# A hybrid SSD and attention layer: the scan's steps in three pieces, the norm per four chunks, GpSimd's products on VectorE and ScalarE

## The chip, the cores and the metric

The kernel runs on one core of a Trainium2 chip. The metric is the device time of one execution in microseconds (us). The engines are named as in the profile: PE is TensorE, DVE is VectorE, ACT is ScalarE, POOL is GpSimd, SP is SyncE, which issues most transfers. PE can run at two clocks, 1.2 and 2.4 GHz; the profile gives the granted clock as a share of the higher one.

## What is computed

One layer of a decoder for 512 tokens of width 1,024 in float32: a gated feed-forward, a mixer, a second gated feed-forward. The mixer projects the normed input once, onto the parts z, xBC and dt of a chunked state-space scan (SSD) and onto q, k and v of a differential attention; both results, side by side, go through an output projection. The change concerns the scan. It works on 4 chunks of 128 tokens, 2 groups of 8 heads of 64 columns:

```python
a_cs = jnp.cumsum(dt * a.reshape(g, hg), axis=2)
xdt = xs * dt[..., None]
seg = a_cs[:, :, :, None] - a_cs[:, :, None, :]
decay = jnp.where(causal, jnp.exp(jnp.where(causal, seg, 0.0)), 0.0)
cb = jnp.einsum("bcign,bcjgn->bcijg", cm, bm)
y_diag = jnp.einsum("bcijgh,bcjghp->bcighp", cb[..., None] * decay, xdt)
decay_states = jnp.exp(a_cs[:, :, -1:] - a_cs)
states = jnp.einsum("bclgn,bclgh,bclghp->bcghpn", bm, decay_states, xdt)
...
_, prev = lax.scan(step, h0, (jnp.moveaxis(states, 1, 0), jnp.moveaxis(chunk_decay, 1, 0)))
y_off = jnp.einsum("bclgn,bcghpn,bclgh->bclghp", cm, prev, jnp.exp(a_cs))
y = y_diag + y_off + xs * d_skip.astype(jnp.float32).reshape(g, hg)[:, :, None]
...
gated = (y_ssd * jax.nn.silu(z.astype(f32))).reshape(bsz, s, SSD_GROUPS, SSD_WIDTH // SSD_GROUPS)
y_ssd = rms_norm(gated, ssd_norm_w[l].reshape(SSD_GROUPS, -1)).reshape(bsz, s, SSD_WIDTH)
```

## The kernel before

Three stages follow each other: the first feed-forward, the mixer, and the second feed-forward. Every weight is split into a high and a low part when it is loaded: SP transfers a piece of 128x1024 (`raw`, three buffers), ACT rounds it to the high part (`whi`, L128), DVE subtracts to get the low part (`wlo`, L129), and a product takes three matmuls (high by high, high by low, low by high). `piece()` (L159) hands out the next piece and loads two ahead.

In the mixer, first the xBC columns are projected, convolved (DVE) and transposed (`conv_tr`). Then comes the stage that the change is about, from the first z matmul at 440 us to the first qk matmul at 581 us. In it PE works through eight projections of 256 columns (`tok_proj`, L590), four for z and four for v. Each has four units, one per block of 128 tokens, of 24 matmuls each, and yields after each unit. Two units share a PSUM bank (tag J, two banks); after the second, the callback empties the bank: for z ACT takes a tanh (L619) and a scaled copy (L620) per block and DVE a product (L621), for v ACT a scaled copy (L629) and DVE a subtraction (L630).

The scan has eight steps (chunk c, group g), the four chunks of group 0 first. They are laid between the units:

- `ssd_a` (L634): SP loads the cumulated decays of eight heads, spread over all partitions (`ab`, 128x8x128, three buffers, L639). PE makes C times B (L641), DVE masks it (`cbm`, L643). DVE subtracts and clamps the decay for each head (L645, eight instructions), ACT takes Exp of all of it (L647). POOL makes `xdt` (L650), the product of decay and `cbm` (L651), `xdd` (L655) and the skip product `y` (L657).
- `ssd_b` (L660): PE multiplies C with the running state (L666), DVE scales it (`yo`, L668), POOL adds it to `y` (L669). PE makes the chunk's state from `xdd` (L672), DVE updates the running state (L677, L678). PE makes the products within the chunk, eight heads (L680, into the other bank of the same tile `pd`), DVE adds `y` (L681) and multiplies with silu(z) (L683). Then comes the norm of this chunk: ACT squares and sums (L685), DVE takes the inverse root in a bit trick and three Newton rounds of three small instructions (`rsqrt`, L207, with L215 to L217) on one value per partition, and scales (L690).
- `ssd_c` (L693): PE transposes the step's result (`yt`, L697), ACT copies it (L698, one buffer), SP stores it in DRAM (`ysave`, L699). It is called one step after `ssd_b`; the last one after the first qk unit (`last_ssd`).

The list `plan` (L702) says within which projection a step stands; `ssd_a` of a step stands just ahead of `ssd_b` of the step before. The order of instructions on each engine is not simply that of the text: the kernel is built with `schedule_with_timeline_sim=True`, and a planner takes what is next in the text and, where its own estimate of times says that this isn't ready yet, something later that is. Each engine then works in that fixed order. After the stage the pools of the scan are closed, and the attention's tiles take their place in SBUF; the first is the square of the qk projection (L749).

## Time and profile before

| | us |
|---|---|
| median of 3 runs | 1207.35 |
| lowest, highest run | 1206.51, 1207.97 |
| span of the profiled execution, first to last instruction | 1203.1 |
| PE busy | 1163.4 |
| DVE busy | 926.0 |
| ACT busy | 533.8 |
| POOL busy | 210.6 |
| transferred | 119.56 MB, 99 GB/s on average |

The profile is of one execution; its own time on the device is not given apart from its span, and the runs are 3.4 to 4.9 us longer than the span. The page lists busy times over the whole span. PE is at 97% of it, but its records are modelled and overlap, so a full PE is not PE at its peak. The sections on stages are read from windows of the trace, in us from the start of the span. An idle time of an engine is put down to the instruction whose end released it.

### The profile page before, as it was taken

The numbers are of one execution on the slowest core, as the hardware profiler recorded it, in microseconds if no ns is written. First come the engines' busy times: TensorE is split into PE (matmuls) and PEld (weight loads), VectorE is DVE, ScalarE is ACT, GpSimd is POOL, SyncE is SP. The second block draws the span as 40 slices with busy tenths as digits, with TensorE's granted clock in tenths as the row PEclk, the third lists the DMA queues.
The fourth block names the chain that finished last, engine by engine and source line by source line (L and its number), as shares of the span: only waits on it lengthen the run. The fifth ranks groups of instructions, "written<-read, shape, count | busy, mean of one in ns | idle before, by whom it ended". The sixth has DMA issues, their size and how long they took to land.

```text
span 1203.1 us, 19035 instructions
## 1 busy us (share of the span) xinstructions
PE 1163.4 (97%) x7483; PEld 1036.3 (86%) x7483; DVE 926.0 (77%) x1593; ACT 533.8 (44%) x863; POOL 210.6 (18%) x214
## 2 busy tenths in 40 slices
PE   8999999999989999798999998899999999999998
PEld 6889999999967788797998886688789999999997
DVE  6988787787585867989588989636499988787862
ACT  5534343433352355343366675735244443434331
POOL 1000000000031004443255756315100000000000
PEclk9999999999998999899999999999999999999999
DMA  7223333333353224242321102216312333333332
GB/s 231 86 75 97 110 110 97 99 107 88 97 193 114 77 82 140 81 131 73 105 71 36 58 32 76 75 44 209 98 62 89 109 121 100 101 107 102 96 114 83
DMA packets 42393, 119.56 MB, mean 99 GB/s; under 512 B 4608, under 2 KB 9920, under 8 KB 42304
## 3 DMA queue, kind: packets, MB, share of 16 engines
q1 hardware_dynamic: 41024, 114.15, 30.3%
q0 software_dynamic: 1280, 4.20, 1.0%
q8 instruction: 59, 0.97, 0.3%
q14 instruction: 30, 0.25, 0.1%
HBM read 112.00 MB, written 6.32 MB: 98 GB/s over the span
## 4 chain that ended last, share of the span: by engine, by line
PE 40%; DVE 10%; issue 2%; ACT 2%; POOL 1%; DMA 0%; DVEq 0%; ACTq 0%; POOLq 0%
PE s L327 5%; PE s L326 5%; PE s L328 5%; PE dn L170 3%; PE dn L172 3%; PE dn L171 3%; PE wo L170 2%; PE wo L171 2%; PE wo L172 2%; DVE nmx L813 2%; DVE pe L823 1%; PE gu L170 1%; PE gu L172 1%; PE gu L171 1%; DVE wlo L129 1%
## 5 line engine op out<-in xcount | busy, mean ns | idle before, releaser
L129 DVE TENSOR_TENSOR wlo<-raw,whi 128x1024 fp32r<-128x1024 f32 (+3 forms) x225 | 225.9, 1007 | 120.0 <-ACT whi L128 104.4
L128 ACT CAST whi<-raw 128x1024 fp32r<-128x1024 f32 (+2 forms) x204 | 175.7, 865 | 310.2 <-PE s L327 121.7
L327 PE MATMUL s<-al,whi 128*128 128x256 f32 x952 | 265.2, 280 | 0.0
L326 PE MATMUL s<-ah,whi 128*128 128x256 f32 x952 | 263.6, 279 | 0.0
L328 PE MATMUL s<-ah,wlo 128*128 128x256 f32 x952 | 262.6, 279 | 0.0
L327 PEld LDWEIGHTS s<-al,whi 128*128 128x128 f32 x952 | 178.7, 188 | 2.1
L326 PEld LDWEIGHTS s<-ah,whi 128*128 128x128 f32 x952 | 178.5, 188 | 2.0
L328 PEld LDWEIGHTS s<-ah,wlo 128*128 128x128 f32 x952 | 177.2, 187 | 0.1
L170 PE MATMUL dn<-h,whi 128*128 128x512 f32 x352 | 137.6, 394 | 0.0
L172 PE MATMUL dn<-h,wlo 128*128 128x512 f32 x352 | 137.5, 392 | 0.0
L171 PE MATMUL dn<-h,whi 128*128 128x512 f32 x352 | 136.9, 389 | 0.0
L128 ACT CAST whi<-tw 128x1024 fp32r<-128x1024 f32 x68 | 70.3, 1049 | 141.2 <-PE s L327 65.7
L129 DVE TENSOR_TENSOR wlo<-tw,whi 128x1024 fp32r<-128x1024 f32 x68 | 82.1, 1220 | 2.8 <-ACT whi L128 2.5
L172 PEld LDWEIGHTS dn<-h,wlo 128*128 128x128 f32 x352 | 66.1, 188 | 14.6
L171 PEld LDWEIGHTS dn<-h,whi 128*128 128x128 f32 x352 | 66.1, 188 | 12.7
L170 PEld LDWEIGHTS dn<-h,whi 128*128 128x128 f32 x352 | 66.1, 188 | 12.2
L603 PE MATMUL qk<-whi,xhm 128*128 128x256 f32 x256 | 73.3, 287 | 1.1 <-DVE l L820 1.1
L605 PE MATMUL qk<-whi,xlm 128*128 128x256 f32 x256 | 72.8, 285 | 0.0
L604 PE MATMUL qk<-wlo,xhm 128*128 128x256 f32 x256 | 72.7, 284 | 0.0
L362 DVE SCALAR_TENSOR_TENSOR x<-dn,x 128x512 f32<-128x512 f32 x64 | 44.0, 688 | 35.4 <-PE dn L172 34.9
L170 PE MATMUL gu<-xh,whi 128*128 128x512 f32 x160 | 64.9, 406 | 2.7 <-POOL whi L126 1.7
L419 POOL DMA_DIRECT2D xsave<-x x8 | 4.6, 578 | 337.3 <-DVE x L362 337.3
(293 smaller groups left out, 2650.8 us busy)
## 6 DMA issues: line engine op xcount, KB each, us to landing
raw<-in_gu SPq DMA_DIRECT2D x86, 512.0 KB, 3.6
raw<-in_dn SPq DMA_DIRECT2D x48, 384.0 KB, 3.2
raw<-in_wqk SPq DMA_DIRECT2D x16, 512.0 KB, 3.6
raw<-in_wxbc SPq DMA_DIRECT2D x12, 512.0 KB, 3.5
raw<-in_wo SPq DMA_DIRECT2D x10, 512.0 KB, 4.1
raw<-in_dn SPq DMA_DIRECT2D x16, 256.0 KB, 2.7
raw<-in_wz SPq DMA_DIRECT2D x8, 512.0 KB, 3.5
ab<-acs_d SPq DMA_DIRECT2D x8, 512.0 KB, 4.1
```

Of the source, the lines that this page charges most:

```text
L128: S.copy(hi[:, a:b], raw[:, a:b])
L129: V.tensor_sub(lo[:, a:b], raw[:, a:b], hi[:, a:b].bitcast(F32))
L170: PE.matmul(ps, lhsT=hi, rhs=xh, start=start, stop=False)
L171: PE.matmul(ps, lhsT=hi, rhs=xl, start=False, stop=False)
L172: PE.matmul(ps, lhsT=lo, rhs=xh, start=False, stop=stop)
L326: PE.matmul(ps, lhsT=hi, rhs=ah[:, i, a], start=i == 0, stop=False)
L327: PE.matmul(ps, lhsT=hi, rhs=al[:, i, a], start=False, stop=False)
L328: PE.matmul(ps, lhsT=lo, rhs=ah[:, i, a], start=False, stop=i == 3)
L362: V.scalar_tensor_tensor(x[d], ps, 0.5, x[d], op0=ALU.mult, op1=ALU.add)
L603: PE.matmul(o, lhsT=xh, rhs=hi, start=k == 0, stop=False)
L604: PE.matmul(o, lhsT=xh, rhs=lo, start=False, stop=False)
L605: PE.matmul(o, lhsT=xl, rhs=hi, start=False, stop=k == KD - 1)
```

## The change

It leaves the mathematics as it is and touches the stage in four ways.

1. `ssd_b` becomes `ssd_o` (product with the state, state update), `ssd_d` (products within the chunk, product with silu(z), sum of squares) and `ssd_n` (norm). A loop over the eight steps runs `ssd_o`, one unit, `ssd_a` of the next step, one unit, `ssd_d`, one unit. Ahead of it stand four units, behind it the remaining four.
2. The norm is taken once per group, after its fourth chunk: one inverse root of four values per partition, and four scalings. The transposes of group 0 come in rounds 5 and 6 of the loop, counted from 0, two chunks in each, those of group 1 in `last_ssd`. `yt` has two buffers.
3. POOL has no work in the stage any more: `xdt`, the decay product, `xdd` and the sum of `y` and `yo` go to DVE. The skip product goes to ACT as eight scaled copies of 128x64. The subtraction and clamp of the decay go from DVE to ACT as eight Relus of the negated difference, and Exp takes the negative of that.
4. The projections are taken in the order z0, z1, v0, z2, z3, v1, v2, v3, and their weights are loaded in that order.

Lines of the text (comments and docstrings) that are removed elsewhere stand for nothing in the program and are left out here.

```diff
@@ -103,8 +103,8 @@
     mixp = [(wxbc[t], 1024) for t in (8, 9, 10, 11)]
     mixp += [(wdt, 128)]
     mixp += [(wxbc[t], 1024) for t in range(8)]
-    mixp += [(wz[g, i], 1024) for g in range(4) for i in range(2)]
-    mixp += [(wv[g, i], 1024) for g in range(4) for i in range(2)]
+    for w, g in ((wz, 0), (wz, 1), (wv, 0), (wz, 2), (wz, 3), (wv, 1), (wv, 2), (wv, 3)):
+        mixp += [(w[g, i], 1024) for i in range(2)]
     mixp += [(wqk[h, i], 1024) for h in range(8) for i in range(2)]
     for ds in ((0, 1), (2, 3), (4, 5)):
         mixp += [(wo[d, 0], 1024) for d in ds] + [(wo[d, 1, :, 0:512], 512) for d in ds]
...
@@ -631,7 +631,10 @@
                                        h.bitcast(F32), op0=ALU.mult, op1=ALU.subtract)
         return tok_proj(f"v{g}", cb)
 
+    ssq = [ssd.tile([P, NB], F32, name=f"ssq{g}") for g in range(2)]
+
     def ssd_a(c, g):
+
         hs = slice(g * 8, g * 8 + 8)
         sh = [P, 8, 64]
         cs = slice(c * P, (c + 1) * P)
...
@@ -642,31 +645,34 @@
         cbm = sb.tile([P, P], F32, tag="cbm", name="cbm")
         V.tensor_mul(cbm, pcb[:, :P], triu)
         for h in range(8):
-            V.tensor_scalar(ab[:, h, :], ab[:, h, :], acs[:, c, g * 8 + h:g * 8 + h + 1], 0.0,
-                            op0=ALU.subtract, op1=ALU.min)
-        S.activation(ab, ab, AF.Exp)
+            S.activation(ab[:, h, :], ab[:, h, :], AF.Relu, bias=acs[:, c, g * 8 + h:g * 8 + h + 1], scale=-1.0)
+        S.activation(ab, ab, AF.Exp, scale=-1.0)
         xg = sview(xs[:, c, g * 512:(g + 1) * 512])
         xdt = sb.tile(sh, F32, tag="xdt", name="xdt")
-        G.tensor_tensor(xdt, xg, dts[:, c, hs].unsqueeze(2).to_broadcast(sh), op=ALU.mult)
-        G.tensor_tensor(ab, ab, cbm.unsqueeze(1).to_broadcast([P, 8, P]), op=ALU.mult)
+        V.tensor_tensor(xdt, xg, dts[:, c, hs].unsqueeze(2).to_broadcast(sh), op=ALU.mult)
+        V.tensor_tensor(ab, ab, cbm.unsqueeze(1).to_broadcast([P, 8, P]), op=ALU.mult)
         xdd = None
         if c < NB - 1:
             xdd = sb.tile(sh, F32, tag="xdd", name="xdd", bufs=1)
-            G.tensor_tensor(xdd, xdt, dsd[:, c, hs].unsqueeze(2).to_broadcast(sh), op=ALU.mult)
+            V.tensor_tensor(xdd, xdt, dsd[:, c, hs].unsqueeze(2).to_broadcast(sh), op=ALU.mult)
         y = sb.tile(sh, F32, tag="y", name="y")
-        G.tensor_tensor(y, xg, row[:, R_DS + g * 8:R_DS + g * 8 + 8].unsqueeze(2).to_broadcast(sh), op=ALU.mult)
+        for h in range(8):
+            S.activation(y[:, h, :], xg[:, h, :], AF.Copy, scale=row[:, R_DS + g * 8 + h:R_DS + g * 8 + h + 1])
         return ab, xdt, xdd, y
 
-    def ssd_b(c, g, m, xdt, xdd, y):
+    pds = {}
+
+    def ssd_o(c, g, m, xdt, xdd, y):
+
         hs = slice(g * 8, g * 8 + 8)
         sh = [P, 8, 64]
         cs = slice(c * P, (c + 1) * P)
-        pd = pA(f"pd{c}{g}")
+        pd = pds[c, g] = pA(f"pd{c}{g}")
         if c > 0:
             PE.matmul(pd[:, 1, :], lhsT=cT[:, g, cs], rhs=state[:, g, :], start=True, stop=True)
             yo = sb.tile(sh, F32, tag="yo", name="yo", bufs=1)
             V.tensor_tensor(yo, sview(pd[:, 1, :]), ea[:, c, hs].unsqueeze(2).to_broadcast(sh), op=ALU.mult)
-            G.tensor_add(y, y, yo)
+            V.tensor_add(y, y, yo)
         if c < NB - 1:
             pst = pM(f"st{c}{g}")
             PE.matmul(pst, lhsT=btok[:, c, g, :], rhs=xdd.rearrange("p a b -> p (a b)"), start=True, stop=True)
...
@@ -676,22 +682,30 @@
             else:
                 V.tensor_tensor(st, st, cdec[:, c, hs].unsqueeze(2).to_broadcast(sh), op=ALU.mult)
                 V.tensor_add(st, sview(pst), st)
+
+    def ssd_d(c, g, m, xdt, xdd, y):
+
+        pd = pds.pop((c, g))
         for h in range(8):
             PE.matmul(pd[:, 0, h * 64:(h + 1) * 64], lhsT=m[:, h, :], rhs=xdt[:, h, :], start=True, stop=True)
         V.tensor_tensor(y, sview(pd[:, 0, :]), y, op=ALU.add)
         zt = sview(sz[:, c, g * 512:(g + 1) * 512])
         V.tensor_mul(zt, zt, y)
-        ss = tiny.tile([P, 1], F32, tag="ss", name=f"ss{c}")
-        S.activation(y, zt, AF.Square, accum_out=ss)
-        V.tensor_scalar(ss, ss, 1.0 / 512, EPS, op0=ALU.mult, op1=ALU.add)
-        rr = tiny.tile([P, 1], F32, tag="ssr", name="ssr")
-        rsqrt(rr, ss, [P, 1], "s")
+        S.activation(y, zt, AF.Square, accum_out=ssq[g][:, c:c + 1])
+
+    def ssd_n(g):
+
+        ss = tiny.tile([P, NB], F32, tag="ss", name=f"ss{g}")
+        V.tensor_scalar(ss, ssq[g], 1.0 / 512, EPS, op0=ALU.mult, op1=ALU.add)
+        rr = tiny.tile([P, NB], F32, tag="ssr", name="ssr")
+        rsqrt(rr, ss, [P, NB], "s")
         sl = slice(g * 512, (g + 1) * 512)
-        V.scalar_tensor_tensor(sz[:, c, sl], sz[:, c, sl], rr, row[:, R_SN + g * 512:R_SN + (g + 1) * 512],
-                               op0=ALU.mult, op1=ALU.mult)
+        for c in range(NB):
+            V.scalar_tensor_tensor(sz[:, c, sl], sz[:, c, sl], rr[:, c:c + 1], row[:, R_SN + g * 512:R_SN + (g + 1) * 512],
+                                   op0=ALU.mult, op1=ALU.mult)
 
     def ssd_c(c, g):
-        yt = sb.tile([P, 4, P], F32, tag="yt", name="yt", bufs=1)
+        yt = sb.tile([P, 4, P], F32, tag="yt", name="yt")
         pt = pM(f"yt{c}{g}")
         for i in range(4):
             PE.transpose(blk(pt, i), sz[:, c, g * 512 + i * P:g * 512 + (i + 1) * P], ident)
...
@@ -699,40 +713,48 @@
         nc.sync.dma_start(ysave[:, g * 4:g * 4 + 4, c, :], yt)
 
     steps = [(c, g) for g in range(2) for c in range(NB)]
-    plan = [[], [], [0, 1], [2], [3], [4, 5], [6], [7]]
-    fills = [z_group(g) for g in range(4)] + [v_group(g) for g in range(4)]
-    st_a = {}
-    done_c = [0]
-
-    def drain_c(upto):
-        while done_c[0] < upto:
-            ssd_c(*steps[done_c[0]])
-            done_c[0] += 1
-
-    for n, fill in enumerate(fills):
-        next(fill)
-        if n == 0:
-            for t, dst in last_conv:
-                conv_tr(t, dst)
-            cv_cm.__exit__(None, None, None)
-            sb_cm = tc.tile_pool(name="ssdb", bufs=2)
-            sb = sb_cm.__enter__()
-            next(fill)
-            st_a[0] = ssd_a(*steps[0])
-            st_a[1] = None
-        for s in plan[n]:
-            next(fill, None)
-            if st_a.get(s + 1) is None and s + 1 < 8:
-                st_a[s + 1] = ssd_a(*steps[s + 1])
-            ssd_b(*steps[s], *st_a[s])
-            drain_c(s)
-        for _ in fill:
-            pass
-    last_ssd = lambda: drain_c(8)
-
-    # ---------------- attention ----------------
+    units = [z_group(0), z_group(1), v_group(0), z_group(2), z_group(3), v_group(1), v_group(2), v_group(3)]
+
+    def unit(n=1):
+
+        while n and units:
+            try:
+                next(units[0])
+                n -= 1
+            except StopIteration:
+                units.pop(0)
+
+    unit()
+    for t, dst in last_conv:
+        conv_tr(t, dst)
+    cv_cm.__exit__(None, None, None)
+    sb_cm = tc.tile_pool(name="ssdb", bufs=2)
+    sb = sb_cm.__enter__()
+    unit()
+    ops = ssd_a(*steps[0])
+    unit(2)
+    for n, s in enumerate(steps):
+        ssd_o(*s, *ops)
+        unit()
+        nxt = ssd_a(*steps[n + 1]) if n < 7 else None
+        unit()
+        ssd_d(*s, *ops)
+        ops = nxt
+        if s[0] == NB - 1:
+            ssd_n(s[1])
+        if n in (5, 6):
+            for c in (0, 1) if n == 5 else (2, 3):
+                ssd_c(c, 0)
+        unit()
+    unit(32)
+
+    def last_ssd():
+        for c in range(NB):
+            ssd_c(c, 1)
+
+
     def rsqrt_act(dst, v, shape):
-        """dst = v ** -0.5: exp(-ln(v) / 2) and a Newton step."""
+
         y = tiny.tile(shape, F32, tag="ra_y", name="ra_y")
         t = tiny.tile(shape, F32, tag="ra_t", name="ra_t")
         S.activation(y, v, AF.Ln)
```

## Rows read from the trace of the kernel before

**Rows 1.** Page, part 1: busy us, share of the span and instructions by engine.
```profile
PE 1163.4 (97%) x7483; PEld 1036.3 (86%) x7483; DVE 926.0 (77%) x1593; ACT 533.8 (44%) x863; POOL 210.6 (18%) x214
```

**Rows 2.** Windows of the SSD stage: length, busy us by engine, granted clock, DMA.
```profile
440.00:581.00 141.00, 126.55 (x988) 119.32 (x987) 115.89 (x250) 57.37 (x103) 53.79 (x37) 0.96 0.31 100
...
440.00:475.00 35.00, 33.59 (x287) 32.53 (x285) 27.39 (x50) 20.11 (x35) 12.37 (x10) 1.00 0.29 96
...
510.00:545.00 35.00, 33.96 (x275) 31.85 (x274) 29.45 (x77) 17.10 (x30) 15.83 (x11) 1.00 0.37 114
```

**Rows 3.** Waits of PE, 440 to 581: us in total, times, longest.
```profile
PE yt L697 <- DVE sz L690: 8.1, 4, 4.1
PE pd L680 <- DVE yo L668: 4.9, 1, 4.9
PE z L603 <- ACT sz L620: 1.3, 1, 1.3
```

**Rows 4.** Windows of one wait and the stretch behind it (columns as in rows 2).
```profile
482.75:487.65 4.90, 0.01 (x2) 0.01 (x1) 4.90 (x10) 0.49 (x1) 3.34 (x2) 0.99 0.00 0
487.65:492.00 4.35, 4.35 (x20) 4.35 (x21) 4.28 (x8) 3.90 (x7) 2.24 (x2) 0.50 0.02 4
```

**Rows 5.** Timeline, 542 to 556: start, us, instruction, [idle before <-releaser].
```profile
542.08 0.68 DVE L668 TENSOR_TENSOR yo<-pd,ea 128x512 f32<-128x512 f32 x1
542.17 2.38 POOL L651 TENSOR_TENSOR ab<-ab,cbm 128x1024 f32<-128x1024 f32 x1 [1.86 <-DVE rs_t L215]
542.68 2.42 DVE L677 TENSOR_TENSOR state<-state,cdec 128x512 f32<-128x512 f32 x1
543.03 1.89 PE L680 MATMUL pd<-xdt,ab 128*128 128x64 f32 x16
...
556.09 0.38 PE L641 MATMUL cb<-cT,bT 128*128 128x128 f32 x2
```

**Rows 6.** Groups by line on DVE, 440 to 581: count | busy us, mean ns | idle before.
```profile
L645 DVE TENSOR_SCALAR ab<-ab,acs 128x128 f32<-128x128 f32 x64 | 26.1, 469 | 3.0 <-DMA ab<-acs_d 3.0
L129 DVE TENSOR_TENSOR wlo<-raw,whi 128x1024 fp32r<-128x1024 f32 x16 | 19.4, 1220 | 3.5 <-ACT whi L128 3.5
L215 DVE TENSOR_TENSOR rs_t<-rs_y 128x1 f32<-128x1 f32 x21 | 10.2, 485 | 0.5
...
L216 DVE SCALAR_TENSOR_TENSOR rs_t<-rs_t,ss 128x1 f32<-128x1 f32 x21 | 7.1, 337 | 0.4
L217 DVE SCALAR_TENSOR_TENSOR rs_y<-rs_t,rs_y 128x1 f32<-128x1 f32 x14 | 7.1, 504 | 0.2
...
L683 DVE TENSOR_TENSOR sz<-sz,y 128x512 f32<-128x512 f32 x8 | 5.7, 710 | 0.2
```

**Rows 7.** One line on DVE: count, shortest/median/longest ns, first and last start.
```profile
L215 DVE TENSOR_TENSOR rs_t<-rs_y x33: 145/160/2092, 29.0 to 863.9; 128x1 f32<-128x1 f32 x24, 128x4 f32<-128x4 f32 x9
```

**Rows 8.** Groups by line on POOL, 440 to 581 (columns as in rows 6).
```profile
L651 POOL TENSOR_TENSOR ab<-ab,cbm 128x1024 f32<-128x1024 f32 x8 | 20.5, 2569 | 22.1 <-DVE cbm L643 9.0 <-DVE rs_t L216 5.1 <-ACT ab L647 5.1
```

**Rows 9.** Groups by line on ACT, 440 to 600 (columns as in rows 6).
```profile
L128 ACT CAST whi<-raw 128x1024 fp32r<-128x1024 f32 x17 | 17.7, 1047 | 8.1 <-PE v L605 6.2 <-PE xbc L171 1.9
...
L629 ACT ACTIVATE vh<-v,rm 128x256 fp32r<-128x256 f32 x16 | 7.5, 471 | 16.8 <-DVE vl L630 12.2 <-PE v L605 4.6
```

**Rows 10.** Timeline of ACT, two instructions in a row (columns as in rows 5).
```profile
452.44 0.48 ACT L619 ACTIVATE th<-z,hr 128x256 f32<-128x256 f32 x1
452.81 0.48 ACT L620 ACTIVATE sz<-z,hr 128x256 f32<-128x256 f32 x1
```

**Rows 11.** Window of four z units without a wait (columns as in rows 2).
```profile
454.06:465.05 10.99, 10.99 (x96) 10.99 (x97) 10.99 (x23) 5.85 (x9) 6.87 (x5) 1.00 0.62 207
```

**Rows 12.** Timeline of SP's queue: the last issue for the scan.
```profile
533.58 0.33 SPq L639 DMA_DIRECT2D ab<-acs_d  x1
```

**Rows 13.** Page, part 6: DMA issues, KB each, median us to landing.
```profile
ab<-acs_d SPq DMA_DIRECT2D x8, 512.0 KB, 4.1
```

**Rows 14.** Timeline of ACT after the stage (columns as in rows 5).
```profile
593.38 0.60 ACT L749 ACTIVATE sqk<-qk 128x512 f32<-128x512 f32 x1 [1.14 <-DMA ysave<-yt]
```

## The prediction

> **What bounds the kernel now.** I read the page first: TensorE is busy 97% of the span [rows 1], so a change pays only where PE waits or runs slowly. All that is changed lies between the first z projection (440 us) and the first qk projection (581 us), so the second view is the window of those 141 us [rows 2]: PE is busy 126.55 us of it, idle 14.45, and its granted clock is 0.96 on average. The third view says what ended the idle time [rows 3]. 8.1 us of PE's waits are transposes of the normed scan output (yt, L697) that wait for the norm's last product on DVE (L690); 4.9 us are the intra-chunk products (pd, L680), put down to DVE's read of the inter-chunk product (yo, L668); 1.3 us are z matmuls that wait for ACT to empty their bank. A wait costs twice: in the 4.9 us of that pd wait PE does nothing while DVE works throughout, and in the 4.35 us behind it the granted clock is 0.50, the 1.2 GHz level, until it is back at 2.4 [rows 4].
>
> Why DVE is late shows in the timeline [rows 5]. While GpSimd multiplies the decay matrix (L651, 2.38 us from 542.17), DVE's L668, which reads PSUM, takes its 0.68 us, but L677, the same size with both inputs in SBUF, takes 2.42 and ends with GpSimd's instruction. The groups say the same of the sums [rows 6, 7]: L215, two SBUF inputs of one element per partition, has a median of 160 ns and a mean of 485; L645's mean is 469 ns for 128 elements, when a product of 512 (L683) takes 710. So the scan's steps hang on a busy DVE that GpSimd holds up, and PE waits at the end of that chain.
>
> **The change, part by part.** The matmuls and transposes are the same in number and shape, so PE's own work stays. What can be won is the idle time and the slow clock: 14.45 us, and 141 x 0.04 = 5.6 us of clock, together **20.1 us**.
>
> GpSimd's five products of a step leave it. DVE takes xdt (8), xdd (6) and y+yo (6), 20 products of 128x512 at L683's 0.71 us = 14.2 us, and the decay product, 8 at 1.22 us (L129, the same size, both inputs in SBUF) = 9.8 us [rows 6]; on GpSimd the latter took 2.57 [rows 8]. Together +24.0 us on DVE.
>
> The subtract-and-clamp of the decay (L645, 64 pieces, 26.1 us) leaves DVE; ACT does it as 64 Relus, and takes the skip product y as 64 copies of 128x64 with a scale. No row shows ACT at these sizes with a per-partition operand from SBUF alone. From L629 (256 elements, 471 ns) and L128 (1,024 elements, 1,047 ns) an element costs 0.75 ns [rows 9], so the far end is 375 ns for 128 and 327 ns for 64. The near end: of two instructions in a row the second starts 0.37 us after the first, which lasts 0.48 [rows 10], so 0.11 us less, 265 and 217 ns. ACT gains 64 x 0.48 = 31 us at the near end, 64 x 0.70 = 45 at the far end; I take the near one, since the eight stand in a row. ACT's 57.4 us become 88 (102 at the worst) [rows 2]; in some 125 us that is 71 to 82%.
>
> By the rows the Relu is no longer on ACT than its predecessor on DVE, 265 to 375 ns against L645's mean of 469 [rows 6], and it lands on the engine with room. A rule of the Trainium skill speaks against the move: "ScalarE: Activation LUTs", section Rules for kernel authors, wants relu on VectorE, up to about three times as fast per element in bf16. The trace doesn't agree in f32; by that factor the sum would be a slowdown (last rival).
>
> The norm is taken per four chunks: seven of the eight Newton chains lie in the stage, 10.2 + 7.1 + 7.1 us in the three groups of [rows 6]. Two chains stay, nine instructions each at the median 160 ns [rows 7], 2.9 us: -21.5 us. The four scalings with L690 stay. DVE's sum: 115.9 - 26.1 - 21.5 + 24.0 = 92 us, 74% of 125 where it was 82%, and nothing locks it out any more, since GpSimd has no work left in the stage.
>
> Now the waits. The transposes of the first group move two steps behind their norm, those of the second behind all of v3; the 8.1 us go. pd comes two projection units behind yo; four units last 10.99 us without a wait, so one lasts 2.75 [rows 11], and 5.5 us cover yo's 0.68 [rows 5]: the 4.9 us go. What is late next is ACT: its z and v banks (the 1.3 us) and the decay chain. What stays of idle time I take from the two quarters of the stage that have no long wait: 1.41 and 1.04 us in 35 [rows 2], 1.23 on average, so 4.4 us in 125. Both ends: nothing stays, or the rivals below.
>
> New waits and what is queued behind them. On SP the four transfers of ysave for the second group come together behind v3's weights. The copies have two buffers where they had one, so the third copy waits on ACT for the first transfer, and ACT's first qk squares stand behind it; they wait for the last transfer already now, and start at 593.38 [rows 14], 12.4 us after the stage. After the change: a qk unit 2.75, then twice a copy (0.6) and a transfer (at most the 4.1 of a larger one [rows 13]), 12.2 us. No change, and PE has four qk units (11 us) and two more under it; if that cover fails, the loss is the difference, under 1 us. The transfer of the decay rows (ab) is issued as soon as one of three buffers is free: the last at 533.58 [rows 12], 22.5 us ahead of its step's first product at 556.09 [rows 5]; I cost it at nothing. The regrouped weight order moves no transfer by more than some units; nothing.
>
> The sum: -14.45 - 5.6 + 4.4 = **-15.7 us**. The profiled execution has a span of 1203.1 us; the median of the runs is 1207.35, 4.25 above, for what lies around it. 1207.35 - 15.7 = 1191.7.
>
> **The rivals.**
> ACT late with the banks (1200 us). In a step ACT has, in one block, 8 Relus, Exp (1.05, as L128's size) and 8 copies, 4.9 to 6.7 us, and at a group's start two weight casts, 2.1: 7.0 to 8.8 us in which no bank is emptied. PE covers two units, 5.5, and the scan's own products, 1.9 (pd) to 2.3: 7.4 to 7.8. So 0 to 1.4 us a step, up to 11 in eight steps, with slow clock behind some: 1187.3 + 11 + 2 = 1200. For it: the 1.3 us of today. Against: the planner puts ready work between. Chance 0.14.
>
> The split does not take effect (1199 us). The order on each engine is the planner's, not the text's; it may bring pd next to yo again. Then only the norm's waits go, and 4.9 us with 2.2 of slow clock [rows 4] stay: 1191.7 + 7.1. Against: DVE is lighter. Chance 0.07.
>
> Slower (1222 us): the state update waits for xdd. In the text DVE's order is xdt, decay product, xdd, and the decay product waits for Exp and that for eight Relus; the state matmul of the step needs xdd. Now GpSimd has that order in its own queue, and none of PE's waits is for it [rows 3]. From Relu to xdd: 2.1 to 3.0 + 1.05 + 1.22 + 0.71 = 5.1 to 6.0 us; behind four bank reads (1.5) and two casts (2.1) 8.7 to 9.6. The cover to the state matmul is unit, pd, unit: 2.75 + 1.89 + 2.75 = 7.4. So 1.3 to 2.2 us a step, in six steps; if the ab transfer is late as well, its 4.1 come on top, 5.4 to 6.3, some 35 us: 1207.35 - 20.1 + 35 = 1222. It decides from 20.1 / 6 = 3.35 us a step on. Against: the transfer's lead of 22.5 us, and that Relus can start as soon as it has landed. Chance 0.10.
>
> ACT as the bound (1234 us). If a Relu took three times L645's 0.469 us, 1.41, the 64 would need 90 us and ACT 57.4 + 90 + 21 (copies at the far end) = 168 us, 27 more than the stage has now: 1207.35 + 27. It decides from 0.8 us a Relu on, where ACT passes the stage's 125 us. Against: both ends for a Relu, 0.265 and 0.375. Chance 0.01. That is what the rule on relu in "ScalarE: Activation LUTs" would come to.
>
> **How the numbers follow.** Forecast 0.66, ACT late 0.14, split undone 0.07, slower 0.11 (0.10 and 0.01), about as before 0.02. The likeliest gives 1191.7. The low end is the whole 20.1 us, 1187; the high end takes in the second and third case, 1202. Beyond it lie the slower cases and the worst of ACT. A measurement here can tell 0.2% (2.4 us) from no change: faster 0.84, same 0.05, slower 0.11.
>
> **What would show it.** Right: the stage from the first z to the first qk matmul is 124 to 127 us long, PE's idle time in it under 6 us, its granted clock 0.99 or 1.00; no wait of the yt transposes for the norm; GpSimd empty; DVE's Newton steps at about 0.16 us on average; ACT between 85 and 102 us. Wrong: PE waits for z or v banks that ACT empties, for xdd or the decay product, with clock at 0.50 behind; or Relus over 0.4 us a piece; or qk products that wait for ysave's transfers.

## The result and the profile after

| | before | after |
|---|---|---|
| median of 4 runs, us | 1206.93 | 1195.41 |
| lowest, highest run | 1206.06, 1207.97 | 1191.88, 1196.45 |
| profiled execution: span (time) | 1203.1 | 1192.3 (1194.4) |
| first z to first qk matmul ("scan") | 140.21 | 121.31 |
| first qk to first matmul of the second feed-forward ("attention") | 273.58 | 281.01 |

The ratio of the runs is 0.9899, with a 95% interval of 0.9882 to 0.9917: faster by 1.0%, inside the range, 3.7 us above the forecast of 1191.7. The two lower lines tell more than the sum: the scan got 18.9 us shorter, and the attention, whose text the change doesn't touch, got 7.4 us longer.

The page after, part 1, answers to [rows 1]: DVE and POOL lost 31 and 55 us of work, ACT gained 36.

```profile
PE 1160.0 (97%) x7483; PEld 1033.1 (87%) x7483; DVE 895.1 (75%) x1485; ACT 569.6 (48%) x991; POOL 155.2 (13%) x178
```

The windows of the two stretches; first the attention before, then both after (columns as in [rows 2]):

```profile
580.84:854.42 273.58, 260.62 (x1735) 226.62 (x1733) 201.51 (x401) 159.00 (x375) 133.60 (x129) 0.99 0.26 81
```

```profile
441.33:562.64 121.31, 119.40 (x977) 112.95 (x976) 87.30 (x154) 89.61 (x231) 0.00 (x0) 1.00 0.34 109
562.64:843.65 281.01, 263.53 (x1739) 229.23 (x1738) 199.22 (x388) 161.32 (x375) 132.59 (x129) 0.99 0.25 81
```

In the scan PE's idle time fell from 14.45 to 1.91 us, its clock is 1.00 throughout, and POOL has nothing to do, against 53.8 us in [rows 2]. In the attention PE's idle time rose from 12.96 (273.58 - 260.62) to 17.48 us, and its busy time from 260.6 to 263.5, though of matmuls only four more transposes of the scan's result lie in it (eight instead of four).

PE's waits in the scan after (us in total, times, longest), against [rows 3]:

```profile
PE pd L690 <- DVE ab L653: 0.8, 1, 0.8
PE z L603 <- ACT sz L620: 0.7, 1, 0.7
PE st L678 <- ACT sz L620: 0.4, 1, 0.4
```

The transposes' 8.1 us and the 4.9 us of pd behind yo are gone; what is left are three short waits. The groups on DVE and on ACT in the same stretch (columns as in [rows 6]):

```profile
L653 DVE TENSOR_TENSOR ab<-ab,cbm 128x1024 f32<-128x1024 f32 x8 | 9.8, 1222 | 5.1 <-ACT ab L649 5.0
...
L215 DVE TENSOR_TENSOR rs_t<-rs_y 128x4 f32<-128x4 f32 x6 | 1.0, 161 | 0.2
```

```profile
L648 ACT ACTIVATE ab<-ab,acs 128x128 f32<-128x128 f32 x64 | 20.4, 416 | 0.3 <-DMA ab<-acs_d 0.3
...
L660 ACT ACTIVATE y<-xs,row 128x64 f32<-128x64 f32 x64 | 16.7, 355 | 0.1
```

L215 has a mean of 161 ns where [rows 6] had 485 (there on one value per partition, which takes 156 ns in move_only below). An instruction of DVE that lasts longer while POOL works is called held from here on. The decay product takes 1.22 us where GpSimd took 2.57 [rows 8]. The Relus last 416 ns each but 20.4 us together, so they start 0.32 us apart on average; the scaled copies 355 ns and 0.26.

### The profile page after: what moved, and what is told of

It reads as the page before. It is cut to its first block, busy times and chain, and to the rows that moved or that the text cites. A ratio compares the mean times of both kernels' runs of the same rounds, so it can differ in the third digit from the quotient of the medians.

```text
span 1192.3 us, 18991 instructions
## 1 busy us (share of the span) xinstructions
PE 1160.0 (97%) x7483; PEld 1033.1 (87%) x7483; DVE 895.1 (75%) x1485; ACT 569.6 (48%) x991; POOL 155.2 (13%) x178
## 4 chain that ended last, share of the span: by engine, by line
PE 83%; DVE 8%; ACT 4%; issue 2%; POOL 1%; DMA 1%; SPq 0%; ACTq 0%; POOLq 0%; DVEq 0%
PE s L327 9%; PE s L326 9%; PE s L328 9%; PE dn L170 6%; PE dn L172 6%; PE dn L171 6%; PE gu L170 3%; PE gu L172 3%; PE gu L171 3%; PE wo L172 2%; PE wo L170 2%; PE wo L171 2%; PE xbc L170 2%; PE xbc L171 2%; PE xbc L172 2%
## 5 line engine op out<-in xcount | busy, mean ns | idle before, releaser
L128 ACT CAST whi<-raw 128x1024 fp32r<-128x1024 f32 (+2 forms) x204 | 176.6, 868 | 309.5 <-PE s L327 121.7
L171 PEld LDWEIGHTS dn<-h,whi 128*128 128x128 f32 x352 | 66.1, 188 | 12.7
L170 PEld LDWEIGHTS dn<-h,whi 128*128 128x128 f32 x352 | 66.1, 188 | 12.2
L172 PE MATMUL gu<-xh,wlo 128*128 128x512 f32 x160 | 63.7, 398 | 0.0
```

Of the source, the lines that this page charges most:

```text
L128: S.copy(hi[:, a:b], raw[:, a:b])
L170: PE.matmul(ps, lhsT=hi, rhs=xh, start=start, stop=False)
L171: PE.matmul(ps, lhsT=hi, rhs=xl, start=False, stop=False)
L172: PE.matmul(ps, lhsT=lo, rhs=xh, start=False, stop=stop)
```

## The experiments

Each experiment gives the windows of scan and attention in that order, and the ratio of its runs to runs of the kernel before on the same occasion. Those had medians of 1204.80 us (the first four kernels below), 1207.33 (the next three), 1207.95 (the next three) and 1205.70 (the last two), so times from different occasions are not compared to the microsecond. The changed kernel, run once more on another occasion:

> The changed kernel once more, on the same chip as the three parts. Stretch from first z to first qk 121 to 122 us, from first qk to the second feed-forward's first matmul 279 to 285 us where it was 273.6 before. If runs differ as much as the first four (1191.9 to 1196.5), the place where this execution differs from the first in the trace is in the attention (a wait and the slow clock behind it), not in the scan.

```profile
438.32:559.55 121.23, 119.40 (x977) 112.94 (x976) 87.30 (x154) 89.27 (x231) 0.00 (x0) 1.00 0.34 109
559.55:843.12 283.57, 266.72 (x1739) 231.85 (x1738) 198.67 (x388) 161.05 (x375) 132.53 (x129) 0.98 0.25 81
```

Run 1197.64 us, ratio 0.9946 (0.9929 to 0.9963): here the change is worth 0.5%, 7.2 us, and this interval doesn't meet that of the first result. The scan repeats to 0.1 us. The attention is 2.6 us longer than in the first execution, as expected, but by slow clock and not by longer waits: PE's idle time in it is 16.85 us, 0.6 less, its busy time 3.2 more, and from 38 to 60 us behind the first qk matmul the clock is 0.92 where the first execution had 1.00. Not expected was that the scan begins 3.0 us earlier (438.32 against 441.33). So spans of single executions differ by some us ahead of the change and behind it, and parts are compared by stretch.

**One part at a time.** First the moved work alone, then everything but the moved work, then the norm per group alone.

```diff
 # move_only: the kernel before with
-V.tensor_scalar(ab[:, h, :], ab[:, h, :], acs[...], 0.0, op0=ALU.subtract, op1=ALU.min)
+S.activation(ab[:, h, :], ab[:, h, :], AF.Relu, bias=acs[...], scale=-1.0)
...
-G.tensor_tensor(xdt, ...); G.tensor_tensor(ab, ab, cbm...); G.tensor_tensor(xdd, ...); G.tensor_add(y, y, yo)
+V.tensor_tensor(xdt, ...); V.tensor_tensor(ab, ab, cbm...); V.tensor_tensor(xdd, ...); V.tensor_add(y, y, yo)
-G.tensor_tensor(y, xg, row[...])
+S.activation(y[:, h, :], xg[:, h, :], AF.Copy, scale=row[...])
```

> Part 3 of the change alone: GpSimd's products on DVE, clamp and skip product on ACT; steps and norm as before. Theory A (DVE, held by GpSimd, makes PE wait; the split only adds cover): DVE's Newton steps fall to 0.16 us, PE's idle time from first z to first qk falls from 14.45 to 4 to 8 us, that stretch from 140.2 to 126 to 131 us; run 1196 to 1201. Rival B (the waits come from the place of yo and of the norm in the order, whoever makes the products): idle stays over 10 us, stretch 134 to 140, run 1202 or more.

```profile
438.88:561.97 123.09, 120.55 (x981) 114.20 (x980) 92.20 (x213) 89.92 (x231) 0.00 (x0) 1.00 0.35 114
561.97:837.19 275.22, 262.75 (x1735) 228.80 (x1733) 201.69 (x401) 159.28 (x375) 133.01 (x129) 0.98 0.26 80
```

Run 1187.74 us, ratio 0.9865 (0.985 to 0.988): this part alone is faster than the whole change on the same occasion (1197.64). It takes 17.1 of the 18.9 us out of the scan, more than theory A expected (123.1 us, where it had 126 to 131). The attention takes 275.2 us; its instructions on DVE and ACT come in the same order as before, one by one. Rival B is out: yo and pd are in one step as before (in the second step PE has about one projection unit between their matmuls, before and now), the norm is taken per chunk, and PE idles 2.5 us.

```diff
 # split_keep_pool: the changed kernel with
-S.activation(ab[:, h, :], ..., AF.Relu, ...)
+V.tensor_scalar(ab[:, h, :], ..., op0=ALU.subtract, op1=ALU.min)
-V.tensor_tensor(xdt, ...)
+G.tensor_tensor(xdt, ...)
...
```

> The changed kernel with part 3 undone: GpSimd keeps its five products, DVE the clamp; steps in three pieces, norm per group. Theory A: DVE is still held (Newton steps and L677-like updates over 0.3 us on average), stretch from first z to first qk 125 to 132 us, run 1199 to 1204. Rival B: stretch 121 to 124, as with the whole change; run 1193 to 1197.

```profile
439.25:568.46 129.21, 123.91 (x978) 116.97 (x976) 106.17 (x190) 56.36 (x103) 59.00 (x36) 0.97 0.32 103
568.46:851.15 282.69, 265.26 (x1739) 230.11 (x1738) 199.47 (x388) 161.03 (x375) 132.38 (x129) 0.98 0.26 81
```

Run 1201.78 us, ratio 0.9976 (0.996 to 0.9992). As A expected: the pieces and the norm per group take 11.0 us out of the scan while GpSimd still holds DVE. In its DVE groups products with two SBUF inputs are held, the gate of 256 elements (L621) at 775 ns and the product with silu(z) at 1,056; in the changed kernel they take 421 and 686. Not every instruction meets GpSimd: of the Newton steps L216 takes 532 ns, L215 158.

```profile
L621 DVE SCALAR_TENSOR_TENSOR sz<-th,sz 128x256 f32<-128x256 f32 x16 | 11.9, 775 | 7.0 <-ACT sz L620 7.0
L693 DVE TENSOR_TENSOR sz<-sz,y 128x512 f32<-128x512 f32 x8 | 8.4, 1056 | 0.2
...
L216 DVE SCALAR_TENSOR_TENSOR rs_t<-rs_t,ss 128x4 f32<-128x4 f32 x6 | 3.2, 532 | 0.2
...
L215 DVE TENSOR_TENSOR rs_t<-rs_y 128x4 f32<-128x4 f32 x6 | 0.9, 158 | 0.1
```

```diff
 # norm_only: the kernel before with
-ss = tiny.tile([P, 1], ...); S.activation(y, zt, AF.Square, accum_out=ss); ...; rsqrt(rr, ss, [P, 1], "s"); ...
+S.activation(y, zt, AF.Square, accum_out=ssq[g][:, c:c + 1])
...
-            drain_c(s)
+            if s in (3, 7):
+                ssd_n(s // 4)
+            if s in (5, 6):
+                drain_c(2 * s - 8)
```

> The norm per group and its transposes later, alone; ssd_b whole, GpSimd's products where they were. Theory A: the 8.1 us of transposes waiting for the norm go, with some slow clock; the 4.9 us of pd behind yo stay: stretch 130 to 134 us, run 1199 to 1203. Rival B (each wait that goes comes back at the next instruction that needs DVE): stretch 136 to 140, run 1204 to 1207.

```profile
440.94:574.09 133.15, 124.19 (x969) 117.31 (x968) 99.06 (x174) 55.29 (x100) 54.70 (x36) 0.96 0.31 99
574.09:856.99 282.90, 267.14 (x1746) 232.35 (x1745) 204.77 (x404) 162.66 (x378) 134.30 (x129) 0.97 0.26 81
```

```profile
PE pd L682 <- DVE yo L670: 7.5, 2, 3.9
```

Run 1209.58 us, ratio 1.0044 (1.0028 to 1.0059): slower, outside both expectations. The scan is as A had it, 133.15, though the waits of pd behind yo grew from 4.9 to 7.5 us (second fence), which is what rival B had in mind; but the attention is 9.3 us longer than before. That is a first hint that the transposes left behind the scan cost something there.

**What the attention gives back.** In the text of the changed kernel all four chunks of the second group are transposed behind the first qk unit (the planner put two of them right ahead of it, at 561.85 us, the other two at 566.27). Two kernels leave only one there, as before; a third leaves four there, with the moved work alone.

```diff
 # after_early_yt: the changed kernel with
-    unit(32)
+    unit(3)
+    ssd_c(0, 1)
+    ssd_c(1, 1)
+    unit()
+    ssd_c(2, 1)
+    unit(32)
...
-        for c in range(NB):
-            ssd_c(c, 1)
+        ssd_c(NB - 1, 1)
```

> The changed kernel, but three of the second group's four chunks are transposed between the last v units; one is left behind the first qk unit, as before. Theory G (the four transposes, copies and transfers behind the first qk unit cost the attention 7 to 9 us): scan 121 to 124 us, first qk to second feed-forward 273 to 277, run 1185 to 1190. Rival H (the planner lays out the attention anew whenever the scan ends otherwise, and the old layout was simply better): 279 us or more there, run 1193 to 1198.

```profile
441.15:562.87 121.72, 119.89 (x981) 113.43 (x980) 86.97 (x154) 90.02 (x232) 0.00 (x0) 1.00 0.34 113
562.87:838.77 275.90, 263.12 (x1736) 229.02 (x1734) 201.12 (x388) 159.70 (x374) 134.45 (x129) 0.99 0.25 81
```

Run 1189.59 us, ratio 0.9855 (0.9838 to 0.9873). The scan takes 121.7 us, and the attention is back at 275.9, as theory G had it.

```diff
 # after_step_norm: the changed kernel with
-S.activation(y, zt, AF.Square, accum_out=ssq[g][:, c:c + 1])
+ss = tiny.tile([P, 1], ...); S.activation(y, zt, AF.Square, accum_out=ss); ...; rsqrt(rr, ss, [P, 1], "s"); ...
...
+        if n:
+            ssd_c(*steps[n - 1])
```

> The changed kernel with the norm per chunk again and each chunk transposed one step later, as before; three pieces and the moved work stay. Theory G: attention 273 to 277 us; scan 122 to 126 (six more Newton chains on DVE, unheld at 0.16 us an instruction), run 1187 to 1192. Rival H: attention 279 us or more, run 1193 or more.

```profile
439.21:568.53 129.32, 123.75 (x982) 117.16 (x980) 96.00 (x226) 90.53 (x232) 0.00 (x0) 0.97 0.34 109
568.53:844.62 276.09, 261.71 (x1734) 227.86 (x1733) 201.87 (x388) 159.16 (x373) 134.07 (x129) 0.99 0.25 80
```

```profile
PE z L603 <- DVE vl L630: 3.7, 1, 3.7
```

Run 1195.02 us, ratio 0.99 (0.9881 to 0.9918). The attention is at 276.1, again as G had it. The scan missed, and with it the run: 129.3 us, the longest of the kernels whose GpSimd is idle, with one wait of 3.7 us for DVE to read a v bank and a clock of 0.97. With the norm per chunk the three pieces are worse than the old order (123.1 in the moved work alone), so the order of pieces and projections can still cost 6 us when nothing holds DVE.

```diff
 # move_late_yt: move_only with
-            drain_c(s)
+            drain_c(min(s, 4))
-yt = sb.tile([P, 4, P], F32, tag="yt", name="yt", bufs=1)
+yt = sb.tile([P, 4, P], F32, tag="yt", name="yt")
```

> The moved work alone, norm per chunk, but the transposes of the second group's four chunks all stand behind the first qk unit, with two buffers for the copies. Theory G: scan 122 to 124 us, attention 280 to 284 instead of 275.2, run 1192 to 1197. Rival H predicts no size; if the attention stays at 273 to 277, G is wrong and the split itself disturbs the attention.

```profile
440.43:562.66 122.23, 119.67 (x971) 113.29 (x970) 92.31 (x213) 88.08 (x228) 0.00 (x0) 1.00 0.33 108
562.66:836.72 274.06, 262.18 (x1744) 228.70 (x1743) 198.60 (x401) 162.00 (x378) 128.52 (x129) 0.99 0.26 83
```

Run 1186.68 us, ratio 0.983 (0.9813 to 0.9847). Here four chunks are transposed late and the attention takes 274.1 us: G falls as a rule. So does H, that the old order was simply better: here and in after_early_yt DVE and ACT work in other orders than before, and the attention is as short. What fits all runs is that the length goes with the order that the planner makes of what follows. With the order of before on DVE and ACT the attention takes 273.6, 275.2 and (in move_clamp_dve below) 274.7 us; split_keep_pool has the changed kernel's order on both, and the three executions with it take 281.0, 283.6 and 282.7. Where this order costs shows in the trace of the changed kernel, at the attention's start (timeline of ACT, POOL, DVE and PE in order of time):

```profile
573.65 0.60 ACT L771 ACTIVATE sqk<-qk 128x512 f32<-128x512 f32 x1 [1.09 <-DMA ysave<-yt]
...
576.53 2.05 POOL L126 TENSOR_SCALAR whi<-raw 128x1024 fp32r<-128x1024 f32 x2
576.62 0.97 DVE L763 SCALAR_TENSOR_TENSOR ra_t<-ra_t,qss 128x8 f32<-128x8 f32 x1
577.62 0.98 DVE L764 SCALAR_TENSOR_TENSOR qrs<-ra_t,ra_y 128x8 f32<-128x8 f32 x1
578.64 0.42 DVE L781 TENSOR_TENSOR kf<-qk,qrs 128x256 f32<-128x256 f32 x1
579.10 0.63 ACT L791 CAST kh<-kf 128x512 fp32r<-128x512 f32 x1 [3.00 <-DVE kf L781]
579.62 0.59 ACT L771 ACTIVATE sqk<-qk 128x512 f32<-128x512 f32 x1
...
581.78 1.22 POOL L789 TENSOR_TENSOR qs<-qf,qs 128x256 fp32r<-128x256 f32 x1 [0.45 <-ACT qs L788]
...
583.05 0.36 PE L810 MATMUL qT<-identr,qs 128*128 128x128 f32 x2 [2.20 <-POOL qs L789]
```

The first qk square starts at 573.65, 11.0 us after the first qk matmul; before it was 12.5 us, so the tiles open no later. But ACT's order is then square, qs, the small steps, kh, and only behind kh the square of the second half (579.62). kh needs DVE's kf (578.64), and two of the three small steps ahead of it (L763, L764; 128x8) take 0.97 and 0.98 us, because POOL rounds two weight pieces beside them (576.53, 2.05 us). So the second qs is late on POOL (581.78), and PE's transposes wait 2.20 us for it. In the kernel before, the two squares stood 1.6 us apart (593.38 in [rows 14], and 594.93), the casts lay ahead of the small steps, and PE didn't wait here. Behind the wait PE runs slowly (first fence the square before, second the window after):

```profile
594.93 0.60 ACT L749 ACTIVATE sqk<-qk 128x512 f32<-128x512 f32 x1 [0.95 <-DVE qss L751]
```

```profile
581.00:600.00 19.00, 16.95 (x136) 16.46 (x136) 12.66 (x27) 7.85 (x22) 8.70 (x9) 0.91 0.29 100
```

A granted clock of 0.91 over 19 us, 1.7 us more. Wait and clock make 3.9 of the 7.4 us; the rest lies in later waits, such as 3.5 us in five waits of the product `at` for DVE's `pe` where before had 0.5 in two, and their cause was not followed. In after_early_yt ACT has the same order here, the second square 5.2 us behind the first, and one small step is still held at 0.97 us; but its first square comes 8.9 us after the first qk matmul instead of 11.0, and no qT transposes wait. So with this order an earlier start seems to help, which is what is left of G. The next experiment takes the casts away from the small steps:

```diff
 # after_act_cast: the changed kernel with
-    pool_hi[0] = True
     for h in range(8):
+        if h == 1:
+            pool_hi[0] = True
         qk_tr(h)
```

> The changed kernel; the weights split while the first head's scores are prepared are rounded by ACT, GpSimd takes over from the second head on. Theory G2 (behind the scan DVE's three small steps of the first qk norm, 454, 970 and 981 ns, are held by two weight casts on GpSimd; that delays kf, kh, the second square and the second qs, for which PE's transposes wait 2.2 us): these steps at 0.17 us, that wait under 1 us, attention 276 to 279 us instead of 281 to 284, run 1189 to 1193. Rival K (ACT, now with the casts, is as late; or a later wait takes the place): attention 280 or more, run 1193 to 1198.

```profile
439.17:560.40 121.23, 119.60 (x977) 113.14 (x976) 87.28 (x154) 89.22 (x231) 0.00 (x0) 1.00 0.34 109
560.40:837.73 277.33, 264.11 (x1740) 230.35 (x1738) 199.78 (x388) 161.78 (x377) 132.46 (x127) 0.98 0.27 82
```

The windows, and of its timeline the two small steps and the transposes that wait:

```profile
574.94 0.17 DVE L763 SCALAR_TENSOR_TENSOR ra_t<-ra_t,qss 128x8 f32<-128x8 f32 x1
575.14 0.17 DVE L764 SCALAR_TENSOR_TENSOR qrs<-ra_t,ra_y 128x8 f32<-128x8 f32 x1
...
579.85 0.36 PE L810 MATMUL qT<-identr,qs 128*128 128x128 f32 x2 [1.23 <-POOL qs L789]
```

Run 1188.35 us, ratio 0.9843 (0.9825 to 0.986). The two steps are at 0.17 us (the first of the three, L762, stays at 0.46), the wait at 1.23 instead of 2.20 (expected under 1), and the attention at 277.3 us, inside what G2 expected: 3.7 us less than in the first execution of the changed kernel, 6.2 less than in the second. That the casts hold the two steps is shown; the edit makes the planner lay out the rest anew too, so how much of the 3.7 us is the held steps is not.

**What of the change is needed.** Two kernels leave further parts out.

```diff
 # move_clamp_dve: move_only with
-S.activation(ab[:, h, :], ab[:, h, :], AF.Relu, bias=acs[...], scale=-1.0)
+V.tensor_scalar(ab[:, h, :], ab[:, h, :], acs[...], 0.0, op0=ALU.subtract, op1=ALU.min)
```

> The moved work alone, but the subtract-and-clamp of the decay stays on DVE (64 pieces, unheld about 0.28 us each): only GpSimd's products and the skip product leave. Theory A: what counts is that GpSimd no longer holds DVE; DVE goes from 93 to 111 us of some 125, ACT from 90 to 70; scan 124 to 128 us, run 1188 to 1193. Rival (DVE at 89% is the bound, the Relus on ACT were needed): scan 130 us or more, run 1195 or more.

```profile
439.32:559.86 120.54, 120.44 (x981) 114.49 (x980) 103.46 (x277) 71.56 (x167) 0.00 (x0) 1.00 0.38 117
559.86:834.56 274.70, 261.47 (x1734) 227.67 (x1733) 201.97 (x401) 159.15 (x375) 133.38 (x129) 0.99 0.26 80
```

```profile
L645 DVE TENSOR_SCALAR ab<-ab,acs 128x128 f32<-128x128 f32 x64 | 13.5, 280 | 2.8 <-DMA ab<-acs_d 2.7
```

Run 1186.77 us, ratio 0.9828 (0.9814 to 0.9843). The scan is the shortest of those seen so far, 120.54 us with 0.10 us idle, below the 124 to 128 of theory A; the rival is out. DVE is busy 103.5 us of it, 86%, and that is no bound. Unheld, a clamp takes 280 ns on DVE (second fence) where the Relu takes 416 on ACT.

```diff
 # move_group_norm: norm_only together with move_only
```

> The moved work and the norm per group, steps not split: what the split itself adds to the two other parts. Theory A: with DVE free, the order of pieces counts for under 2 us: scan 121 to 124 us where the whole change has 121.3. Rival (yo right ahead of pd still costs): scan 126 us or more. The attention's length tells once more whether four transposes behind the first qk unit cost (280 to 284) or not (273 to 277).

```profile
441.03:562.75 121.72, 119.39 (x970) 113.05 (x968) 82.31 (x138) 87.93 (x228) 0.00 (x0) 1.00 0.35 109
562.75:843.08 280.33, 265.36 (x1747) 230.58 (x1745) 203.96 (x404) 161.25 (x378) 131.76 (x129) 0.98 0.26 82
```

Run 1194.24 us, ratio 0.9892 (0.9877 to 0.9907). Without the split the scan takes 121.7 us, with it 121.3: given the two other parts, the split adds 0.4 us. The attention is at 280.3, with four chunks transposed late; its first square comes 19.0 us after the first qk matmul, in move_late_yt 12.7. The two traces show a reason (first fence move_group_norm, second move_late_yt):

```profile
567.77 2.74 DVE L695 SCALAR_TENSOR_TENSOR sz<-sz,ssr,row 128x512 f32<-128x512 f32 x4
...
571.25 0.60 PE L702 MATMUL yt<-ident,sz 128*128 128x128 f32 x4
...
581.77 0.60 ACT L757 ACTIVATE sqk<-qk 128x512 f32<-128x512 f32 x1 [3.86 <-DMA ysave<-yt]
```

```profile
565.50 0.82 PE L697 MATMUL yt<-ident,sz 128*128 128x128 f32 x6
```

The group's norm is taken after its last chunk, so none of the four chunks can be transposed before its scalings, which end at 570.51, 7.8 us after the first qk matmul; with the norm per chunk the first late transposes start after 2.8 us (565.50). No run tried this by itself.

**Two kernels with several of these edits together.**

```diff
 # clamp_act_cast: move_clamp_dve with the edit of after_act_cast
 # early_yt_clamp_cast: after_early_yt with the clamp on DVE and the edit of after_act_cast
```

> GpSimd's products on DVE, skip product on ACT, clamp on DVE, no split, norm per chunk; besides, ACT rounds the weights split while the first head is prepared. If GpSimd's casts hold up the first head in general, the attention shortens from 274.7 to 271 to 273 us and the run from 1186.8 to 1183 to 1186. If they cost only where the planner lays them beside DVE's first small steps, as in the changed kernel, nothing is won: 274 to 277 us, run 1186 to 1189. Scan 120.5 us in both.

```profile
439.37:559.71 120.34, 120.24 (x982) 114.29 (x980) 103.48 (x277) 71.54 (x167) 0.00 (x0) 1.00 0.37 117
559.71:833.17 273.46, 262.68 (x1735) 227.32 (x1733) 200.54 (x401) 161.16 (x377) 128.69 (x127) 0.99 0.26 81
```

Run 1183.82 us, ratio 0.9816 (0.9787 to 0.9844). The attention, 273.5 us, lies between the two expectations, and the interval overlaps that of move_clamp_dve: whether the casts cost anything in the old order is not settled.

> The changed kernel with both repairs of the attention's start (three of four late transposes among the v units, first head's weights rounded by ACT) and the clamp on DVE: whether the split and the norm per group add anything once GpSimd no longer holds DVE. Theory A: nothing; scan 120 to 122 us as without them (120.5), attention 273 to 277, run 1184 to 1189. Rival (they add their 1.8 us also here): scan 118.5 to 119.5, run under 1184.

```profile
438.59:559.26 120.67, 120.09 (x981) 113.83 (x980) 98.55 (x218) 72.12 (x168) 0.00 (x0) 1.00 0.36 114
559.26:832.14 272.88, 261.44 (x1735) 227.22 (x1734) 199.15 (x388) 160.94 (x376) 133.04 (x127) 0.99 0.27 82
```

Run 1182.96 us, ratio 0.9808 (0.9784 to 0.9832), the lowest median, 1.9% below before, but not told apart from clamp_act_cast, whose interval nearly coincides. The run lies 1 us below what theory A expected, on the rival's side; the scan decides between them. Split and norm per group add nothing to it (120.7 against 120.3), as theory A had it.

## Why the prediction was right, and where it wasn't

**The range and the sign** were right because the scan was read rightly: the idle time and the slow clock of one stretch bound the gain at 20.1 us, and 18.9 of them came. That the whole run came within 3.7 us of the forecast is partly luck: the scan won 3.2 us more than the sum, and the attention lost 7.4 that no term had. The range reached up to 1202 for rivals that didn't come. On the second occasion the change was worth 7.2 us where 15.7 were forecast. Of the 4.25 us between span and median only some 2 lie around the execution (1194.4 against a span of 1192.3 after the change); so the profiled execution was probably a quick one, which doesn't touch the difference.

**The cause.** Held DVE as the root was right and is shown by experiment: the moved work alone takes 17.1 us out of the scan, with the norm and yo where they were, and with the clamp left on DVE it takes out 19.7. L215's group falls to 0.16 us wherever POOL is empty. That GpSimd's products were late themselves is no rival: in the kernel before, none of the waits of PE, DVE and ACT that the trace lists in the stage is put down to POOL. The Trainium skill, "SBUF — State Buffer", section SBUF: two separate sides, says it as a rule: an exclusive lock, with the loser fully blocked, between GpSimd and a DVE instruction with two SBUF inputs. The trace agrees: L677 takes 2.42 us beside GpSimd's 2.38, L668, which reads PSUM, its usual 0.68 [rows 5]. L645, which has one SBUF tensor and a value per partition as inputs, is held as well: 469 ns on average before, 280 in move_clamp_dve.

**The parts don't add up.** The steps of the sum took each wait away by its own edit: the norm's by the grouping, pd's by the split. They are substitutes. In the scan the moved work alone is worth 17.1 us, the two others together 11.0 without it, and 1.8 with it. Not every pairing adds something: the split beside the moved work, with the norm per chunk, makes the scan 6.2 us longer (after_step_norm).

**ACT and DVE.** ACT was forecast at 88 us, with 102 at the worst, and measured 89.6; DVE at 92, and measured 87.3. The first came closer than its term: Relus and copies take 37.1 us, where 31 were counted, but ACT's busy time rose by 32.9 only, since three copies of transposes (2 us) left the stage and instructions in a row overlap. The second left out that DVE's other instructions are no longer held, such as L677 (1,112 ns before, 683 after). The near end for a Relu, 265 ns, was too low: one lasts 416 ns, above the 0.4 that was named as a sign of being wrong, and the next starts after 319, between the two ends. "ScalarE: Activation LUTs" of the Trainium skill, section What ACT_TABLE_LOAD costs, gives an estimate of 387 ns for such an instruction (280 + 0.833 x 128) and states an overlap of 93 ns; the trace has 416 and 97. The rule on relu on the same page of the Trainium skill, section Rules for kernel authors, was right in direction: with the clamp on DVE the scan is 2.5 us shorter (120.5 against 123.1), far from the 27 us that the last rival priced. The prediction found the trace against the rule because it took L645's mean of 469 ns for the clamp's own time; but that is the held time: the median in the same trace is 276, and unheld the mean is 280.

**What stays.** Forecast 4.4 us of idle time, measured 1.91: that term was mis-sized by 2.5 us, and the clock came back whole. So the scan, 121.3 us, is shorter than the 124 to 127 that were to show the prediction right. The rival on xdd did not come: no wait is put down to it, the decay product cost 0.8 us once. The rival on banks came with 0.7 us.

**The step that failed** is the one costed at nothing: "No change, and PE has four qk units (11 us) and two more under it; if that cover fails, the loss is the difference, under 1 us." The start of the attention's tiles was forecast at 12.2 us after the stage and measured at 11.0, in part by luck: the first transposes ran ahead of the first qk unit and not behind it, and one transfer took 6.1 us, not at most 4.1. But the cover was asked of the first square alone. What PE needs is the second qs, and between the two lies a chain over three engines whose order the planner made anew. It started 19.1 us after the first qk matmul and was ready at 20.4; its transposes were due at 18.2 and waited 2.20 us. With slow clock and later waits the attention grew by 7.4 us in the one execution and 10.0 in the other; in the first, 3.9 us of it are followed to their cause, and the rest stays open. Forecast scan and attention, -15.7 and 0; measured -18.9 and +7.4, and 0.7 us for a later start: -10.8 of the span.

## What to carry to other kernels

Before splitting or delaying steps around a late engine, ask what makes its instructions long: here taking one engine's work away did more than two reorderings, and made these needless. Where a planner sets the order, a change of one stage lays out the next one anew, so compare by stretches from one first matmul to the next, and try the parts of a change singly; all of them together can be slower than one of them. A cover for a moved transfer has to be checked to the end of the chain that PE waits for, not to its first instruction.

## What the runs showed that I had not expected

- DVE instructions on 128x8 elements are held as long as a whole weight cast of GpSimd: 0.97 and 0.98 us instead of 0.17.
- A norm taken in fewer instructions can lose: grouped alone, it gave 1209.58 us against 1204.80 on the same occasion, with a scan 7.1 us shorter.
- Runs of one kernel lie some us apart (the changed kernel's four from 1191.88 to 1196.45, the kernel before's four within 1.9 then, but fourteen on the second occasion from 1202.12 to 1210.80), and yet the changed kernel's scan agrees to 0.1 us in two executions; the stretches ahead of it and behind it differ by 3.0 and 2.6.
